# Gated linear attention on one core: the gate's split parts stacked as rows of one product, values and output gates as 512-column products, and the mixer's steps in another order

## The chip, the cores and the metric
The kernel runs on one core of a Trainium2 chip. The metric is device time in microseconds (us), the median of three runs; lower is better.

## The reference
A bidirectional encoder of four layers over 256 tokens of width 1024. Each layer is a half-step SwiGLU feed-forward network (FFN, inner width 2816), one mixer, and a second FFN, each with RMSNorm ahead and a residual add behind. The fourth layer's mixer is the one that the change touches, a gated linear attention (GLA) with 4 heads (keys 128 wide, values 256 wide) in both directions:

```python
def _gla_mixer(u, w_in, w_a1, w_a2, b_a, norm_g, w_o):
    proj = u @ w_in
    q, k, v, r = jnp.split(proj, [GLA_DK, 2 * GLA_DK, 2 * GLA_DK + GLA_DV], axis=-1)
    ...
    def log_decay(d):
        z = ((u @ w_a1[d]) @ w_a2[d] + b_a[d]).astype(F32)
        return (jax.nn.log_sigmoid(z) / GLA_TAU).reshape(b, s, GLA_HEADS, GLA_HEAD_K)
    ...
    o = o_fwd + o_bwd
    o = o * lax.rsqrt(jnp.mean(o * o, axis=-1, keepdims=True) + EPS)
    o = o.reshape(b, s, GLA_DV) * norm_g.astype(F32) * jax.nn.silu(r.astype(F32))
    return o.astype(u.dtype) @ w_o
```

`w_a1` is 1024 x 16 and `w_a2` 16 x 512 for each direction; each direction is a scan over chunks of 64 tokens with a masked product inside a chunk.

## The kernel before
**Products.** Every large product is made of float32r parts: an operand is split into a rounded part (ACT, Copy, `split` L634 and `split_block` L167) and the rest (DVE, subtract, L636 and L170), and a product is three matmuls (`mm3`), or in the FFN a 256-column and a 512-column one (`wide`). TensorE (PE) holds 128 x 128 weights and streams 256 or 512 columns.

**Weights.** SP loads blocks of 128 x 2048 numbers (1 MB) into a ring of 4 (`raw`), ACT and DVE split each into a ring of 4 (`w`), the stage's code takes a block with `take`, gives it back with `done`, and `pump` issues the splits that are owed. A new block is loaded when one has been split, so splits, loads and PE's demand move together.

**Order.** There is no planner: each engine works through its instructions in the order in which the code issues them, and a wait stands where the code put it. A tile with a tag has `bufs` buffers; the next tile with the tag waits until the readers of the one that it replaces are done. The eight PSUM banks form two halves of four, here called A0 to A3 and B0 to B3. `ab()` goes round one half and leaves out the banks in `held`; `dbank(j)` names a bank of the other half. The mixer's `bank()` alternates between the two until the output product has begun (`D4`, made by the first `dmm`), which keeps the four `dbank` banks; from there on only the four of `ab()` are left.

**What lies ahead of the mixer.** The FFN before it runs eleven column steps: `take_up("w1", i)` into the banks PA, `take_up("w3", i)` into the banks PB, each evacuated by two ACT copies (`parts`, L466) and two DVE adds (`add`, L471); then DVE multiplies (L474, L480), ACT takes the silu, and the gate's result `g` is split. At i = 4 the code calls `pre3` (L1150), which loads and prepares the mixer's small operands: the gate's first weights `was`, the triangles `tri` and `lst`, `mask`, and the gate's second weights `wa2`. They come through tiles with the tag `craw` (2 buffers), which POOL (GpSimd) clears and fills by DMA and ACT and DVE convert; `wa2` is loaded as it is.

**The mixer** (`mix3`, L1180): `qkproj` 0 to 3 make queries and keys, evacuated by DVE (`qkevac`, L1222 and L1225); the gate's first product with `was` stands between 1 and 2; the four gate products (`gate_a`, L1252, fp32, 17 rows with the bias as a row of ones) stand among the steps of `qkproj(2)`; ACT and DVE turn them into log decays (`gate_b`, `gate_c`). Then each head has `vproj` and `rproj` (8 steps each, one block of weights, one bank; evacuated by ACT, L1289 and L1309) and `decays`, `states`, `scores`, `out`, `trans`, which are spread among these steps by `fill` so that PE has work while ACT and DVE prepare what it needs next. `dmm` is a step of the output product.

## Time and profile before
| | before |
|---|---|
| runs (us) | 1937.98, 1934.15, 1933.92 |
| median (us) | 1934.15 |
| profiled execution (us) | 1937.17 |
| its span (us) | 1935.0 |
| mean granted clock of TensorE, share of full | 0.994 |
| PE busy | 1906.1 us, 99% |
| DVE busy | 1397.5 us, 72% |
| ACT busy | 995.4 us, 51% |
| POOL busy | 35.0 us, 2% |

The page gives for each engine the time in which it executed something, for each group of instructions the mean duration and the idle time of the engine just before them with what ended it, and the chain of work that ended last. The timeline gives single instructions with their start and duration (a run of equal ones is one row with its count; a row's duration runs to the end of its last one). The profiled execution is one run, 3.0 us over the median.

### The profile page before, as it was taken

How to read it: one execution, taken by the hardware profiler on the slowest of the kernel's cores; microseconds unless marked ns; L12 is line 12 of the kernel's file. 1: busy time of each engine (PE TensorE's matmuls, PEld its weight loads, DVE VectorE, ACT ScalarE, POOL GpSimd, SP SyncE). 2: the span in 40 equal slices, each digit the busy share in tenths (PEclk: the TensorE clock that was granted, in tenths of full speed). 3: DMA queues.
4: the chain of work that ended last, by engine and by line, in shares of the span. 5: the costliest groups of instructions: out<-in, count | busy, mean ns of one | idle time of the engine just before them, and what ended most of it. 6: DMA issues, size and time to landing. Idle time of an engine off the chain costs nothing.

```text
span 1935.0 us, 29203 instructions
## 1 busy us (share of the span) xinstructions
PE 1906.1 (99%) x12272; PEld 1683.3 (87%) x12272; DVE 1397.5 (72%) x1850; ACT 995.4 (51%) x1273; POOL 35.0 (2%) x55
## 2 busy tenths in 40 slices
PE   7999999999999999899999999999999999999998
PEld 6888999888888898788888889988888888998886
DVE  7776567876687767787668776687777766768774
ACT  6554444655455544555545544555445455756452
POOL 0000000000040000000000000000000000000000
PEclk9999999999999999899999999999999999999999
DMA  7655533465445543245545544365546553335550
GB/s 264 219 194 193 188 131 131 153 217 196 174 164 212 194 162 144 79 163 216 196 174 196 195 176 164 133 226 183 183 168 220 201 196 111 131 130 193 199 196 22
DMA packets 48644, 338.10 MB, mean 175 GB/s; under 512 B 5568, under 2 KB 5744, under 8 KB 8192
## 3 DMA queue, kind: packets, MB, share of 16 engines
q1 hardware_dynamic: 47952, 335.11, 48.3%
q8 instruction: 96, 1.57, 0.3%
q0 software_dynamic: 560, 1.12, 0.2%
q14 instruction: 36, 0.29, 0.0%
HBM read 335.16 MB, written 1.05 MB: 174 GB/s over the span
## 4 chain that ended last, share of the span: by engine, by line
PE 92%; DVE 5%; ACT 2%; DMA 1%; issue 1%; SPq 0%; DVEq 0%; ACTq 0%
PE B L81 50%; PE A L81 41%; DVE w L170 1%; ACT w L167 1%; DVE zc L765 1%; DMA raw<-in_ffn_w_dram 0%; PE A L84 0%; DMA h<-in_x_dram 0%; ACT zc L880 0%; PE B L84 0%; DVE h L279 0%; DVE acc L355 0%; DVE x L304 0%; DVE sl L474 0%; ACT x L302 0%
## 5 line engine op out<-in xcount | busy, mean ns | idle before, releaser
L170 DVE TENSOR_TENSOR w<-raw,w 128x2048 fp32r<-128x2048 f32 x315 | 720.4, 2293 | 289.7 <-ACT w L167 289.4
L167 ACT ACTIVATE w<-raw 128x2048 fp32r<-128x2048 f32 x315 | 598.8, 1909 | 109.0 <-PE A L81 47.4
L81 PE MATMUL B<-x,w 128*128 128x256 f32 (+1 forms) x3968 | 643.5, 322 | 1.4 <-DVE sl L471 1.2
L81 PEld LDWEIGHTS B<-x,w 128*128 128x128 f32 x3968 | 571.5, 190 | 71.1 <-issue 5.5
L81 PE MATMUL A<-x,w 128*128 128x256 f32 x3008 | 522.4, 335 | 10.9 <-DVE w L636 7.3
L81 PEld LDWEIGHTS A<-x,w 128*128 128x128 f32 x3008 | 455.5, 189 | 74.9 <-DVE w L636 7.3
L81 PE MATMUL B<-g,w 128*128 128x256 f32 (+1 forms) x1408 | 251.1, 336 | 0.3 <-DVE w L170 0.2
L81 PE MATMUL A<-g,w 128*128 128x256 f32 (+1 forms) x1408 | 250.3, 336 | 0.0
L81 PEld LDWEIGHTS B<-g,w 128*128 128x128 f32 x1408 | 216.5, 187 | 32.2 <-DVE g L636 0.5
L81 PEld LDWEIGHTS A<-g,w 128*128 128x128 f32 x1408 | 216.6, 187 | 31.4
L635 ACT ACTIVATE g<-br 128x512 fp32r<-128x512 f32 x88 | 55.6, 632 | 252.9 <-DVE br L480 252.9
L474 DVE TENSOR_TENSOR sl<-sl,R 128x512 f32<-128x512 f32 x176 | 121.9, 696 | 2.5
L636 DVE TENSOR_TENSOR g<-br,g 128x512 fp32r<-128x512 f32 x88 | 61.1, 695 | 61.4 <-ACT g L635 61.4
L302 ACT ACTIVATE x<-h,cols 128x256 fp32r<-128x256 f32 x88 | 39.9, 501 | 68.3 <-DVE h L279 49.0
L466 ACT ACTIVATE br<-B 128x256 f32<-128x256 f32 x88 | 30.3, 385 | 76.3 <-PE B L81 76.3
L477 ACT ACTIVATE sl<-sl 128x512 f32<-128x512 f32 x88 | 55.0, 627 | 24.5 <-DVE sl L474 24.4
L466 ACT ACTIVATE br<-A 128x256 f32<-128x256 f32 x88 | 30.2, 384 | 71.5 <-PE A L81 71.4
L81 PE MATMUL B<-w,x 128*128 128x256 f32 (+1 forms) x504 | 62.6, 284 | 0.0
L81 PEld LDWEIGHTS B<-w,x 128*128 128x128 f32 x504 | 61.3, 191 | 0.4 <-issue 0.3
L480 DVE TENSOR_TENSOR br<-sl,br 128x512 f32<-128x512 f32 x88 | 60.7, 690 | 0.5
L466 ACT ACTIVATE sl<-A 128x256 f32<-128x256 f32 x88 | 29.8, 377 | 53.1 <-PE A L81 53.1
L466 ACT ACTIVATE sl<-B 128x256 f32<-128x256 f32 x88 | 29.9, 378 | 51.5 <-PE B L81 51.1
(293 smaller groups left out, 1088.9 us busy)
## 6 DMA issues: line engine op xcount, KB each, us to landing
raw<-in_ffn_w_dram SPq DMA_DIRECT2D x262, 1024.0 KB, 4.8
raw<-in_attn_w_qk_dram SPq DMA_DIRECT2D x12, 1024.0 KB, 4.8
raw<-in_conv_w_pw_dram SPq DMA_DIRECT2D x12, 1024.0 KB, 4.8
raw<-in_gla_w_in_dram SPq DMA_DIRECT2D x12, 1024.0 KB, 4.8
raw<-in_attn_w_v_dram SPq DMA_DIRECT2D x6, 1024.0 KB, 4.8
raw<-in_fnet_w_dram SPq DMA_DIRECT2D x4, 1024.0 KB, 4.8
raw<-in_gla_w_o_dram SPq DMA_DIRECT2D x4, 1024.0 KB, 4.7
raw<-in_ffn_w_dram SPq DMA_DIRECT2D x8, 256.0 KB, 6.1
```

The source lines that it names most:

```text
L81: return self.nc.tensor.matmul(out, lhsT, rhs, start=start, stop=stop, skip_group_check=True)
L167: self.nc.scalar.activation(w[:, 0], raw, AF.Copy)
L170: (eng or self.nc.vector).tensor_tensor(w[:, 1], raw, f32(w[:, 0]), ALU.subtract)
L302: nc.scalar.activation(xh[:, c], h[:, c], AF.Copy, scale=g[c])
L466: nc.scalar.activation(t[:, c], P[c][:, 1], AF.Copy)
L474: nc.vector.tensor_tensor(t, t, self.Rb(), ALU.mult)
L477: nc.scalar.activation(t, t, AF.Silu)
L480: nc.vector.tensor_tensor(br, sl, br, ALU.mult)
L635: self.nc.scalar.activation(p[:, 0], src, AF.Copy)
L636: self.nc.vector.tensor_tensor(p[:, 1], src, f32(p[:, 0]), ALU.subtract)
L765: nc.vector.scalar_tensor_tensor(o, x, w, o, ALU.mult, ALU.add)
```

## The change
In `pre3` the tag `craw` has one buffer in place of two. `was` has 128 columns in place of 64 (four groups of 32: for each direction the weights twice) and is loaded and split in two halves, each a clearing and four DMAs; `wa2` becomes a pair of float32r parts, 128 x 512, made from a cleared tile with eight small DMAs; it now stands ahead of the triangles and the mask. The gate's input `t1` has 128 rows; its rounded part and rest become the rows of one operand `t2`, so that a gate is two float32r products of 64 and 32 rows in place of one fp32 product of 17 rows. `vproj` and `rproj` become `vrproj`: blocks of 4 x 512 columns (`gla_w_vr`, laid out by the host), two banks per head, 512-column matmuls, 48 per head in place of 96 of 256 columns; values and output gates of a head are evacuated together at its end (L1310, L1313), and the values lie in the space of `was`. The steps are spread by counts (6; then 4, 2, 2; for the last head 12, 4, 6 steps of the output product), and the output product begins right behind the decays of head 3.

```diff
     def pre3(self):
 
         nc, P = self.nc, self.prepool
-        raw = lambda shape: self.sb(self.ev, shape, F32, "craw", 2)
-
-        wa = raw([128, 8, 64])
-        nc.gpsimd.memset(wa, 0.0)
-        for d in range(2):
-            nc.gpsimd.dma_start(wa[:, :, 32 * d:32 * d + 16],
-                                self.a["gla_w_a1"][0, d].rearrange("(k p) n -> p k n", p=128))
+        raw = lambda shape: self.sb(self.ev, shape, F32, "craw", 1)
+
+        was = self.pair(P, [128, 8, 128], "was")
+        cut = [slice(32 * n + 1, 32 * n + 17) for n in range(4)]
+        for ks in (slice(0, 4), slice(4, 8)):
+            wa = raw([128, 4, 128])
+            nc.gpsimd.memset(wa, 0.0)
+            for n, c in enumerate(cut):
+                nc.gpsimd.dma_start(wa[:, :, c],
+                                    self.a["gla_w_a1"][0, n // 2].rearrange("(k p) n -> p k n", p=128)[:, ks])
+            self.split(wa, was[:, :, ks])
+
+        wb = raw([128, 512])
+        nc.gpsimd.memset(wb, 0.0)
+        for n, c in enumerate(cut):
+            nc.gpsimd.dma_start(wb[c, :], self.a["gla_w_a2"][0, n // 2])
+            nc.gpsimd.dma_start(wb[32 * n:32 * n + 1, :], self.a["gla_b_a"][0, n // 2:n // 2 + 1, :])
+        wa2 = self.pair(P, [128, 512], "wa2")
+        self.split(wb, wa2)
         traw = raw([128, 2, 256])
         nc.gpsimd.dma_start(traw, self.a["c_tri"])
-        was = self.pair(P, [128, 8, 64], "was")
-        self.split(wa, was)
         tri = self.sb(P, [128, 2, 256], F32R, "tri")
         nc.scalar.activation(tri, traw, AF.Copy)
         lraw = raw([128, 2, 128])
@@ -1171,10 +1181,6 @@
         nc.scalar.activation(lst, lraw, AF.Copy)
         mask = self.sb(P, [128, 2, 256], mybir.dt.uint8, "mask")
         nc.vector.tensor_copy(mask, mraw)
-        wa2 = self.sb(P, [64, 512], F32, "wa2")
-        for d in range(2):
-            nc.gpsimd.dma_start(wa2[32 * d:32 * d + 16, :], self.a["gla_w_a2"][0, d])
-            nc.gpsimd.dma_start(wa2[32 * d + 16:32 * d + 17, :], self.a["gla_b_a"][0, d:d + 1, :])
         return was, wa2, tri, lst, mask
...
-                self.held = [self.nab]
+                self.held = self.held + [self.nab]
...
         for k in range(8):
-            self.mm3(pa[0:64, 0:256], was[:, :, k], self.xk(k), start=k == 0, stop=k == 7)
+            self.mm3(pa[:, 0:256], was[:, :, k], self.xk(k), start=k == 0, stop=k == 7)
         self.bcast()
-        t1 = T([64, 256])
-        nc.gpsimd.memset(t1, 1.0)
+
+        t1 = T([128, 256])
+        t2 = T([128, 256], F32R, "t2", 1)
+        nc.vector.tensor_tensor(t1, pa[:, 0:256], self.R, ALU.mult)
         for d in range(2):
-            pr = slice(32 * d, 32 * d + 16)
-            nc.vector.tensor_tensor(t1[pr], pa[pr, 0:256], self.R[pr], ALU.mult)
+            nc.gpsimd.memset(t1[64 * d:64 * d + 1], 1.0)
+        nc.scalar.activation(t2, t1, AF.Copy)
+        for d in range(2):
+            pr = slice(64 * d + 32, 64 * d + 64)
+            nc.vector.tensor_tensor(t2[pr], t1[pr], f32(t2[pr]), ALU.subtract)
         qkevac(0, p0)
         qkevac(1, p1)
 
+        v = f32(self.pair(self.prepool, [128, 8, 128], "was")).rearrange("p t a b -> p t (a b)")
+        vt = [v[:, t] for t in range(2)]
+
 
...
         def gate_a(d, t):
-            pr = slice(32 * d, 32 * d + 17)
             p = bank()
-            self.mm(p, t1[pr, 128 * t:128 * t + 128], wa2[pr, :], start=True, stop=True)
+            for n in range(2):
+                pr = slice(64 * d, 64 * d + (64, 32)[n])
+                self.mm(p, t2[pr, 128 * t:128 * t + 128], wa2[pr, n], start=n == 0, stop=n == 1)
             az = self.sb(ev, [128, 512], F32, f"ks{d}{t}")
...
 
-        def vproj(i):
+        rg = {}
+
+        def vrproj(i):
 
             def step(k, s):
+                if k % 4 == 0:
+                    s["w"] = self.take(("gvr", i, k // 4))
                 if k == 0:
-                    s["w"], s["p"] = self.take(("gv", i)), bank(True)
+                    s["p"] = [bank(True) for _ in range(2)]
                 w, p = s["w"], s["p"]
                 for t in range(2):
-                    self.mm3(p[:, 256 * t:256 * t + 256], self.xk(k, t), w[:, :, k],
-                             start=k == 0 and t == 0, stop=k == 7)
+                    x = self.xk(k, t)
+                    for n, (a, b) in enumerate(((0, 0), (0, 1), (1, 0))):
+                        self.mm(p[t], x[:, a], w[:, b, k % 4], start=k == 0 and n == 0, stop=k == 7 and n == 2)
+                if k % 4 == 3:
+                    self.done()
                 if k == 7:
                     self.held = []
-                    self.done()
-                    for t in range(2):
-                        nc.scalar.activation(vt[t][:, 256 * i:256 * i + 256], p[:, 256 * t:256 * t + 256], AF.Copy,
-                                             scale=self.rc[:, t:t + 1])
-            s = {}
-            return [lambda k=k: step(k, s) for k in range(8)]
-
-        rg = {}
-
-        def rproj(i):
-            def step(k, s):
-                if k == 0:
-                    s["w"], s["p"] = self.take(("gr", i)), bank(True)
-                w, p = s["w"], s["p"]
-                for t in range(2):
-                    self.mm3(p[:, 256 * t:256 * t + 256], self.xk(k, t), w[:, :, k],
-                             start=k == 0 and t == 0, stop=k == 7)
-                if k == 7:
-                    self.held = []
-                    self.done()
                     g = self.sb(ev, [128, 2, 256], F32, "rg", 2)
                     for t in range(2):
-                        nc.scalar.activation(g[:, t], p[:, 256 * t:256 * t + 256], AF.Silu, scale=self.rc[:, t:t + 1])
+                        nc.scalar.activation(vt[t][:, 256 * i:256 * i + 256], p[t][:, 0:256], AF.Copy,
+                                             scale=self.rc[:, t:t + 1])
+                    for t in range(2):
+                        nc.scalar.activation(g[:, t], p[t][:, 256:512], AF.Silu, scale=self.rc[:, t:t + 1])
                     rg[i] = g
             s = {}
             return [lambda k=k: step(k, s) for k in range(8)]
@@ -1433,44 +1437,31 @@
             for _ in range(len(steps) if n is None else n):
                 steps.pop(0)()
 
-        fill(vproj(0))
         H = [head(hd) for hd in range(4)]
-        f = rproj(0)
-        fill(f, 4)
+        f = vrproj(0)
+        fill(f, 6)
         kstate()
-        H[0][0]()
         fill(f)
-        H[0][1]()
-        self.pump(1)
-        f = vproj(1)
-        fill(f, 4)
-        H[0][2]()
-        self.pump()
-        fill(f)
-        H[0][3]()
-        for hd in range(1, 4):
+        for hd in range(4):
             decays, states, scores, out, trans = H[hd]
             decays()
             self.pump()
-            f = rproj(hd)
             if hd < 3:
-                fill(f)
-                states()
-                H[hd - 1][4]()
-                f = vproj(hd + 1)
-                fill(f, 4)
-                scores()
+                f = vrproj(hd + 1)
+                n = (4, 2, 2)
             else:
-                fill(f, 4)
-                states()
-                fill(f)
-                scores()
-                H[2][4]()
                 wo = [self.take(("go", j)) for j in range(2)]
                 f = [lambda j=j, k=k, d=d: self.dmm(wo[j], og[j], d, k)
                      for j in range(2) for k in range(2) for d in (4, 5, 6, 7, 0, 1, 2, 3)]
+                n = (12, 4, 6)
+            fill(f, n[0])
+            states()
+            if hd:
+                H[hd - 1][4]()
+            fill(f, n[1])
+            scores()
             self.pump()
-            fill(f, 4)
+            fill(f, n[2])
             out()
         fill(f)
...
+
+    w = a["gla_w_in"][0]
+    o["gla_w_in"] = cols(w[:, :1024], 4)[0]
+    o["gla_w_vr"] = w[:, 1024:].reshape(2, 4, 128, 2, 4, 256).transpose(4, 0, 2, 1, 3, 5).reshape(4, 2, 128, 2048)
```

Three places in the engines' queues. The first is ACT's queue at `pre3`, ahead of the mixer, between the FFN's silu of step 4 (`sl`) and the evacuation of the step's `w3` product (`br`); `DMASW` is a wait for a DMA that POOL issued. Before:

```order
L477 ACTIVATE sl_1008_12792<-sl_1008_12792 128x512 [waits DVE_49]
L635 ACTIVATE was_1013_12810<-craw_1011_12804 128x512 [waits DMASW5_49,DMASW4_49,Pool_49]
L1165 ACTIVATE tri_1014_12813<-craw_1012_12808 128x512 [waits DMASW6_49]
L1171 ACTIVATE lst_1017_12819<-craw_1015_12815 128x256 [waits DMASW7_49]
L466 ACTIVATE br_1020_12860<-A2_71 128x256 [waits PE_49]
L466 ACTIVATE br_1020_12860<-A3_72 128x256 [waits PE_49]
L167 ACTIVATE w_1021_12863<-raw_1000_12667 128x2048 [waits DMAHW5_49,Activation_49]
```

With the change:

```order
L477 ACTIVATE sl_1008_12792<-sl_1008_12792 128x512 [waits DVE_49]
L635 ACTIVATE was_1011_12804<-craw_1012_12805 128x512 [waits DMASW6_49,DMASW5_49,DMASW7_49,DMASW4_49,Pool_49]
L635 ACTIVATE was_1011_12804<-craw_1013_12813 128x512 [waits DMASW2_49,DMASW1_49,DMASW3_49,DMASW0_49,Pool_49]
L635 ACTIVATE wa2_1015_12831<-craw_1014_12821 128x512 [waits DMASW4_49,DMASW3_49,DMASW5_49,DMASW2_49,DMASW6_49,DMASW1_49,DMASW7_49,DMASW0_49,Pool_49]
L1175 ACTIVATE tri_1017_12836<-craw_1016_12834 128x512 [waits DMASW4_49]
L1181 ACTIVATE lst_1020_12842<-craw_1018_12838 128x256 [waits DMASW5_49]
L466 ACTIVATE br_1022_12878<-A2_71 128x256 [waits PE_49]
L466 ACTIVATE br_1022_12878<-A3_72 128x256 [waits PE_49]
L167 ACTIVATE w_1023_12881<-raw_1000_12667 128x2048 [waits DMAHW5_49,Activation_49]
```

Three conversions stood ahead of the evacuation `br`; now five do, each with its own buffer generation of `craw` and its own landing.

The second is PE's queue at head 0, around the decays (`tri` with the log decays `la`); `w` with `x` are the steps of the projections, `lst` and `kT` belong to `kstate`. Before:

```order
L81 MATMUL B0_73<-w_1107_14001,x1_1075_13599 128x256 x12
L84 MATMUL A3_72<-ident_105,kT_1096_13844 128x128 x2
...
L81 MATMUL B3_76<-la11_1116_14088,lst_1017_12819 128x512
L81 MATMUL A2_71<-tri_1014_12813,la00_1113_14079 128x256 [waits Activation_49]
L81 MATMUL A2_71<-tri_1014_12813,la00_1113_14079 128x256
L81 MATMUL A2_71<-tri_1014_12813,la01_1114_14082 128x256 x2
L81 MATMUL B1_74<-tri_1014_12813,la10_1115_14085 128x256 [waits Activation_49]
L81 MATMUL B1_74<-tri_1014_12813,la10_1115_14085 128x256
L81 MATMUL B1_74<-tri_1014_12813,la11_1116_14088 128x256 x2
L81 MATMUL B0_73<-w_1107_14001,x2_1087_13796 128x256 x12
L81 MATMUL B0_73<-w_1107_14001,x3_1089_13824 128x256 x12
L81 MATMUL A3_72<-gv0_1097_13845,ks00_1123_14235 128x256 [waits DVE_49]
```

With the change:

```order
L80 MATMUL A2_71<-w_1106_14016,x0_1076_13599 128x512 [waits Activation_49]
L80 MATMUL A2_71<-w_1106_14016,x0_1076_13599 128x512 x2
L80 MATMUL B0_73<-w_1106_14016,x0_1076_13599 128x512 [waits DVE_49]
L80 MATMUL B0_73<-w_1106_14016,x0_1076_13599 128x512 x2
...
L80 MATMUL B3_76<-la11_1118_14113,lst_1020_12842 128x512
L80 MATMUL A2_71<-w_1108_14021,x3_1091_13842 128x512 x3
L80 MATMUL B0_73<-w_1108_14021,x3_1091_13842 128x512 x3
L80 MATMUL A2_71<-w_1108_14021,x3_1091_13842 128x512 x3
L80 MATMUL B0_73<-w_1108_14021,x3_1091_13842 128x512 x3
L80 MATMUL A2_71<-tri_1017_12836,la00_1115_14104 128x256 [waits Activation_49]
L80 MATMUL A2_71<-tri_1017_12836,la00_1115_14104 128x256
L80 MATMUL A2_71<-tri_1017_12836,la01_1116_14107 128x256 x2
L80 MATMUL B0_73<-tri_1017_12836,la10_1117_14110 128x256 [waits Activation_49]
```

The decays stood in the middle of head 0's output-gate steps (bank B0) and wrote A2 and B1, from which the values had gone long before; now they stand right behind the last step of head 0 and write A2 and B0, the two banks that this step has just filled. The second bank, B0, is also the one of `qkproj(2)`, with a wait for DVE at its first matmul.

The third is PE's queue from the output of head 2 (`P` and `S`) over the decays of head 3 to what follows. Before:

```order
L81 MATMUL A1_70<-S12_1193_14721,E1_1182_14641 64x256
L81 MATMUL B0_73<-tri_1014_12813,la00_1113_14079 128x256 x2
L81 MATMUL B0_73<-tri_1014_12813,la01_1114_14082 128x256 x2
L81 MATMUL A2_71<-tri_1014_12813,la10_1115_14085 128x256 x2
L81 MATMUL A2_71<-tri_1014_12813,la11_1116_14088 128x256 x2
L81 MATMUL B1_74<-w_1170_14563,x0_1074_13581 128x256 x12
L81 MATMUL B1_74<-w_1170_14563,x1_1075_13599 128x256 x12
L81 MATMUL A3_72<-gv0_1097_13845,ks00_1123_14235 128x256 [waits Activation_49]
L81 MATMUL B2_75<-gv0_1097_13845,ks00_1123_14235 128x256
```

With the change:

```order
L80 MATMUL B3_76<-S12_1197_14631,E1_1187_14578 64x256
L80 MATMUL A2_71<-tri_1017_12836,la00_1115_14104 128x256 [waits Activation_49]
L80 MATMUL A2_71<-tri_1017_12836,la00_1115_14104 128x256
L80 MATMUL A2_71<-tri_1017_12836,la01_1116_14107 128x256 x2
L80 MATMUL B0_73<-tri_1017_12836,la10_1117_14110 128x256 x2
L80 MATMUL B0_73<-tri_1017_12836,la11_1118_14113 128x256 x2
L80 MATMUL A2_71<-og0_1159_14411,w_1174_14509 128x256 [waits Activation_49]
L80 MATMUL A2_71<-og0_1159_14411,w_1174_14509 128x256 x5
L80 MATMUL A3_72<-og0_1159_14411,w_1174_14509 128x256 x6
...
L80 MATMUL A3_72<-og0_1159_14411,w_1174_14509 128x256 x6
L80 MATMUL B1_74<-was_1110_14027,ks00_1125_14222 128x256
```

Behind the decays stood four steps of a projection into the free bank B1; now the output product (`og`) starts there, in A2, which the decays have just filled.

## Rows read from the trace of the kernel before

**Rows 1.** The page, part 1: busy time of each engine

```profile
PE 1906.1 (99%) x12272; PEld 1683.3 (87%) x12272; DVE 1397.5 (72%) x1850; ACT 995.4 (51%) x1273; POOL 35.0 (2%) x55
```

**Rows 2.** The page, part 4: the chain that ended last

```profile
PE 92%; DVE 5%; ACT 2%; DMA 1%; issue 1%; SPq 0%; DVEq 0%; ACTq 0%
```

**Rows 3.** Timeline, FFN ahead of the mixer: start, duration, engine, line, out<-in [idle before <-releaser]

```profile
1479.01 0.63 ACT L635 ACTIVATE was<-craw 128x512 fp32r<-128x512 f32 x1
...
1480.85 0.68 DVE L636 TENSOR_TENSOR was<-craw,was 128x512 fp32r<-128x512 f32 x1
...
1481.83 0.54 POOL L1169 DMA_DIRECT2D craw<-in_c_mask_dram  x1 [0.82 <-DVE was L636]
...
1483.35 0.48 POOL L1176 DMA_DIRECT2D wa<-in_gla_w_a_dram  x1
...
1486.76 0.43 DVE L1173 CAST mask<-craw 128x512 uint8<-128x512 f32 x1 [5.22 <-DMA craw<-in_c_mask_dram]
...
1486.98 18.19 PE L81 MATMUL A<-x,w 128*128 128x256 f32 x104
...
1487.70 0.74 DVE L471 TENSOR_TENSOR br<-br,A 128x256 f32<-128x256 f32 x2
...
1495.96 0.74 DVE L471 TENSOR_TENSOR sl<-sl,A 128x256 f32<-128x256 f32 x2
```

**Rows 4.** Timeline, POOL at its first loads for the mixer

```profile
1423.79 0.53 POOL L1156 MEMSET craw<- 128x512 f32 x1 [706.90 <-DVE acc L355]
...
1424.61 1.83 POOL L1158 DMA_DIRECT2D craw<-in_gla_w_a_dram  x2 [0.29 <-POOL craw L1156]
```

**Rows 5.** Windows: length, clock, share of the DMA engines, GB/s

```profile
1484.00:1485.00 1.00, 1.00 1.05 434
```

**Rows 6.** DMA issues, 1400 to 1800 us: KB each, us to landing

```profile
craw<-in_c_mask_dram POOLq DMA_DIRECT2D x1, 256.0 KB, 4.9
craw<-in_gla_w_a_dram POOLq DMA_DIRECT2D x2, 64.0 KB, 3.8
craw<-in_c_tril_dram POOLq DMA_DIRECT2D x1, 128.0 KB, 2.3
```

**Rows 7.** Timeline, a head's 48 matmuls of 256 columns, then `states` and its evacuation

```profile
1684.09 5.91 PE L81 MATMUL A<-w,x 128*128 128x256 f32 x48
...
1689.93 0.48 PE L81 MATMUL B<-gv,ks 64*128 64x256 f32 x1
...
1692.18 0.86 DVE L1376 SCALAR_TENSOR_TENSOR S<-S,dc,B 128x256 f32<-128x256 f32 x2
```

**Rows 8.** Timeline, a gate's product, DVE's evacuations of queries and keys

```profile
1623.26 1.12 PE L81 MATMUL A<-wa,t 17*128 17x512 f32 x2
...
1626.40 0.68 DVE L1222 SCALAR_TENSOR_TENSOR qT<-B,R 128x512 f32<-128x512 f32 x1
...
1639.99 1.28 DVE L1225 TENSOR_TENSOR kT<-B,R 128x512 f32<-128x512 f32 x2
```

**Rows 9.** Windows: length, PE busy, granted clock, share of the DMA engines, GB/s

```profile
1628.40:1632.00 3.60, 3.60 (x9) 0.50 0.71 287
1632.00:1635.20 3.20, 3.20 (x16) 0.50 0.00 0
...
812.60:816.00 3.40, 3.33 (x16) 0.50 0.58 246
```

**Rows 10.** Timeline, PE in the conv mixer, ahead of the last of these windows

```profile
812.29 12.11 PE L81 MATMUL A<-zs,w 128*128 128x256 f32 x84 [2.35 <-ACT zs L635]
```

**Rows 11.** Timeline, heads 0 and 1: output gates, decays behind an output, their evacuation

```profile
1654.93 1.28 ACT L1309 ACT_TABLE_LOAD   x1
...
1656.22 0.84 ACT L1309 ACTIVATE rg<-B,rc 128x256 f32<-128x256 f32 x2
...
1665.15 0.74 PE L81 MATMUL B<-tri,la 128*128 128x256 f32 x4
...
1667.91 0.38 ACT L1351 ACTIVATE Em<-B 128x256 f32<-128x256 f32 x1
```

More of the change, by code (lines that the diff above doesn't have):

```diff
@@ L23 @@
 NW = 4
-GLA_ORDER = [("gv", 0), ("gr", 0), ("gv", 1), ("gr", 1), ("gv", 2), ("gr", 2), ("gv", 3), ("gr", 3)]
 ALL_STAGES = [s for i in range(4) for s in (("ffn", i, 0), ("mix", i), ("ffn", i, 1))]
@@ L141, in plan @@
                     add(("gqk", i), a["gla_w_in"][i], 8)
-                for n, i in GLA_ORDER:
-                    add((n, i), a["gla_w_in"][{"gv": 4, "gr": 8}[n] + i], 8)
+                for i in range(4):
+                    for hf in range(2):
+                        add(("gvr", i, hf), a["gla_w_vr"][i, hf], 4)
                 for j in range(4):
@@ L1204, in mix3 @@
         kT = self.sb(ev, [128, 4, 256], F32, "kT")
-        vt = [self.sb(ev, [128, 1024], F32, f"gv{t}") for t in range(2)]
         def qkproj(i, hook=None):
@@ L1603, in lay @@
     o["conv_w_pw1"] = cols(a["conv_w_pw1"], 8)[0]
-    o["gla_w_in"] = cols(a["gla_w_in"], 12)[0]
+    w = a["gla_w_in"][0]
+    o["gla_w_in"] = cols(w[:, :1024], 4)[0]
+    o["gla_w_vr"] = w[:, 1024:].reshape(2, 4, 128, 2, 4, 256).transpose(4, 0, 2, 1, 3, 5).reshape(4, 2, 128, 2048)
     for n in ("attn_w_o", "conv_w_pw2", "gla_w_o"):
```

## The prediction
> **What bounds the kernel now.** I read the page first: PE is busy for 1906.1 of 1935.0 us [rows 1], and the chain that ended last lies on PE for 92% [rows 2]. So PE's time is the kernel's time: work taken from PE is a gain if PE does not then wait, and every new wait of PE is a loss, whatever DVE (72%) and ACT (51%) have to spare over the whole. The timeline then shows two stretches that the change touches, the FFN step in which `pre3` stands and the mixer. In both I looked for the next event that PE needs and the queue behind which it stands. Two things are to be seen there. ACT and DVE work strictly in their order: DVE stood still for 5.22 us until the mask had landed, although the evacuation of a finished bank (`br`, L471) was behind it [rows 3]. That idle time cost PE nothing: the add began at 1487.70, and PE came to that bank only after 32 more matmuls. And a buffer with the tag `craw` is filled again only when its last reader is done: the mask's DMA waited for DVE's read of `was` [rows 3].
>
> **1. `pre3`, the largest term.** One buffer for six loads makes one chain: clear, load, convert, and only then the next load. The first load has been there for long, as now. From the end of DVE's part of it the chain is, by rows: DVE done 1480.85 + 0.68 = 1481.53 [rows 3]; 0.3 to POOL, a clearing 0.53, 0.29 to the DMA [rows 4]; four DMAs. An issue takes 0.92 for two halves of 64 KB [rows 4] and 0.48 for a small one [rows 3]; for 32 KB I take 0.7, so that the last begins at 1484.75.
>
> The landing is the unknown. Three rows bound it: 2.3 for 128 KB, 3.8 for 64 KB, 4.9 for 256 KB [rows 6]. The size does not order them. The 4.9 fell together with a weight block, while the DMA engines moved 434 GB/s [rows 5]. In the chain no new block is loaded, since blocks are loaded when one has been split and ACT and DVE split nothing while they stand there; only the block on its way until some 1486 is in the way. So I take 2.9 for the second half of `was`, 2.3 for the small ones, 2.65 for the two of 256 KB (2.3 and 128 KB more at that rate), 2.3 for `tril`; together 12.8. If all took 2.3 it would be 11.5, if all took 4.9, 24.5.
>
> The clock goes on: landed 1487.65; ACT 0.63 and DVE 0.68 [rows 3], 1489.0; clearing and hops as above 1490.1; eight DMAs of 0.48, the last begins at 1493.5, landed 1495.8; converted 1497.15; `tri` 0.3 later, landed 1500.1, converted 1500.75; `tril` landed 1503.35, converted (0.4) 1503.8; the mask landed 1506.75, converted by DVE. In the trace `br`'s add began 0.94 after the mask's conversion [rows 3], so now at 1507.7, and its first half is done at 1508.1.
>
> PE's cover: the row of 104 matmuls has 174.9 ns each [rows 3]; the 32 of `w1` end at 1486.98 + 5.6 = 1492.6, and the next one writes the bank that `br` holds. **PE stands for 15.5 us.** Behind it DVE is late: it took 8.26 us from `br`'s add to the next `sl` add [rows 3], PE has only the 5.6 us of `w3` until it needs that bank: 8.26 + 0.37 - 0.4 - 5.6 = 2.6. **Together 18.1** (16.8 to 29.8 by the landings).
>
> **2. The gate.** Four gates lay on PE with 1.12 us each [rows 8]; now each is two 512-column matmuls. The pair of 256 and 512 columns takes 349.8 ns (twice 174.9), the 256-column one 5.84 / 48 = 121.7, from the start of a head's 48 to the start of the next work [rows 7], so a 512-column one 228 and a gate, with the same tail of 0.07, 0.54: -2.3. Besides, PE ran at half clock in both windows from 1628.4 to 1635.2 [rows 9], behind gates that use 17 rows: 6.8 us, 3.4 lost. With 64 and 32 rows in half the time I take this stretch as gone (0 if it comes again): -3.4.
>
> What is late next: the fourth gate writes the bank of `qkproj(1)`, whose evacuation (`qT`, 1626.40, [rows 8]) stands behind two splits of weights on DVE. These now stand behind a longer preparation: one product, a clearing of two rows by POOL, an ACT copy, two DVE subtractions, some 2.1 us more. So the bank is free at about 1629.2, and PE, some 3 us earlier, comes at 1626.9: +2.4. Then the first product of `vrproj(0)` takes B0, the bank of `qkproj(2)`, which DVE frees with `kT` behind all log decays: 1639.99 + 0.64 [rows 8], by my count of ACT's chain 1 us earlier now. Before, the first product went to another bank. PE comes at 1636.3: +3.3. So the gate's gain on PE is given back at once: ACT and DVE set the pace between gate and `kT`.
>
> **3. 512 columns.** Each of eight products of 48 x 256 columns becomes 24 x 512: 5.84 - 24 x 0.228 = 0.37, together -2.9 (0 if a 512-column matmul costs twice a 256-column one). The Trainium skill ("TensorE: Matmul & The Clock Gate", on back-to-back issue at full clock) gives N/2.4 GHz and 2.5 ns; by an estimate from this the two are 109.2 and 215.7 ns, the gain would be 0.5 and my sum 2.4 higher. The trace's 121.7 ns for 256 columns does not agree, and I go by it.
>
> **4. The banks of the new order.** `vrproj` fills two banks, and ACT empties them after the last step in this order: two copies, a table load of 1.28, two silus of 0.42 each [rows 11]. A bank is free with its silu: 0.2 + 0.84 + 1.28 + 0.44 = 2.75 after PE's last matmul, less a little that PE has left: 2.6 for `decays(0)`, which follow directly in A2, and 2.5 each for `out(1)` and `out(2)`, which follow directly in the first bank of the next head's pair; 0.1 for `decays(1)`, which have an output ahead. Before, rg's bank was never the next one wanted. The Trainium skill ("ScalarE: Activation LUTs", what a table load costs) counts 1380 ns of draining besides 1283 for the load; by it each of the three waits would be 1.4 longer. Here the silu begins 1.29 after the load's start, so no row shows it.
>
> Head 3: the first `dmm` writes A2, which the decays have just filled; Em is read 1667.91 + 0.38 - 1665.15 = 3.1 after the decays began [rows 11], PE is there after 1.0: +2.1. `states` now fill all four banks left, and `trans(2)` follows at once: S is done 1692.18 + 0.86 - 1689.93 = 3.1 after the states began [rows 7], which take 1.5: +1.6. `trans(3)` has less output work ahead: +0.7, an estimate. Sum: 2.4 + 3.3 + 2.6 + 0.1 + 2.5 + 2.5 + 2.1 + 1.6 + 0.7 = **17.8**.
>
> **5. The clock.** Behind a wait of 2.35 us [rows 10] PE ran at half clock (1.2 GHz) for 3.4 us [rows 9], 1.7 lost. Part 2 and part 4 bring six waits of that size; I count two such stretches, +3.4 (0 to +10.2). Behind the long wait in the FFN it costs nothing more, since PE waits for DVE there again.
>
> `was` has 128 columns as weights in place of 64 and streams the same 256; the moved `wa2` and POOL's clearing of `t1` are in the chains above. Edits in the host's layout cost nothing: the blocks are of 1 MB and as many as before, behind the same ring.
>
> **The sum.** 18.1 + 17.8 - 2.3 - 3.4 - 2.9 + 3.4 = +30.7. The profiled execution took 1937.17, 3.0 over the median of 1934.15; against its own time this is 1967.9, against the median 1964.9. I predict **1965**; its own range is 1957 to 1975.
>
> **Rivals.**
> - *The loads are as slow as the slowest row.* 4.9 each, 11.7 more: 1977. For it: two of the three landings in the rows are 3.8 and over. Against: a weight block lay beside them. Some of it is likelier than all.
> - *All six waits bring half clock.* 6.8 more: 1972.
> - *`pre3` stays hidden* (the chain runs earlier than I think, or PE has more to do than `w1`): without 18.1, 1947. It decides if `br`'s add ends before 1492.6. Against: ACT's queue holds all five conversions ahead of `br`.
> - *A table load holds ACT 1.4 us longer* in part 4, by its price for draining: three times, 1969. The row above speaks against it.
> - *ACT and DVE keep ahead of PE: faster.* The place is the queues behind each new wait; the price is that of the waits. If every landing and every evacuation were over when PE comes, only the gains were left, 2.3 + 3.4 + 2.9 = 8.6: 1925.5. It decides as soon as the new waits together are under 8.6 us. For it: ACT is busy for half the span only. Against: the silus come behind PE's last matmul into the very bank that PE wants next, whatever ACT did before.
> - *512 columns bring nothing*: 2.9 more, 1968.
>
> **How the numbers follow.** My forecast 0.62; slow landings in full or in part 0.13; half clock everywhere 0.1; hidden `pre3` 0.06; the table load 0.02; no gain from 512 columns 0.04; faster 0.03. The range takes the forecast's own and the cases above it and leaves out the hidden `pre3` and the faster case: 1952 to 1979. A measurement of this kernel tells some 0.2%, 3.9 us, from no change; the forecast lies eight times that away, and only the last big rival lies below. Faster 0.03, same 0.01, slower 0.96.
>
> **What would show it.** Right: ACT and DVE idle for most of 1481 to 1508 with releasers DMA `craw`, POOL with a row of `craw` every few us, PE idle for some 15 us ahead of an A bank in `w3`, released by DVE L471; in the mixer PE idle behind ACT `rg` three times, DVE `qT`, DVE `kT`, ACT `Em`, DVE `S`; no half clock around the gates. Wrong: PE's wait in the FFN under 8 or over 25 us; silu waits under 1 us; a half clock behind every wait.

## The result and the profile after

The changed kernel takes 1966.42 us in the median (1964.64 to 1967.42) against 1934.68 before: a ratio of 1.0159, with a 95% interval of 1.0147 to 1.0172, 31.7 us slower. The forecast was 1965 with a range of 1952 to 1979.

The page of the changed kernel, part 1, shows that PE did as much as before [rows 1] and that only the span grew:

```profile
PE 1906.3 (97%) x12080; PEld 1674.2 (85%) x12080; DVE 1398.7 (71%) x1853; ACT 999.7 (51%) x1278; POOL 42.5 (2%) x68
```

The view of PE's waits, 1400 to 1800 us of the changed kernel, by what ended them (total in us, times, longest), names the waits that the change brought:

```profile
PE A L80 <- DVE br L471: 15.1, 1, 15.1
PE A L80 <- ACT rg L1313: 4.9, 2, 2.6
PE B L80 <- DVE kT L1230: 2.6, 1, 2.6
PE B L80 <- ACT rg L1313: 2.3, 1, 2.3
PE A L80 <- ACT Em L1355: 2.0, 1, 2.0
PE B L83 <- DVE S L1380: 1.8, 1, 1.8
...
PE B L80 <- DVE qT L1227: 0.2, 1, 0.2
```

The same view of the kernel before has one line:

```profile
PE B L81 <- DVE sl L471: 0.2, 1, 0.2
```

The largest stands in the FFN ahead of the mixer. The timeline of the changed kernel there (start, duration, engine, line, out<-in, idle before and its releaser) is the chain that answers to [rows 3]:

```profile
1478.64 0.53 POOL L1159 MEMSET craw<- 128x512 f32 x1 [53.53 <-DVE was L636]
1479.46 2.96 POOL L1161 DMA_DIRECT2D craw<-in_gla_w_a_dram  x4 [0.29 <-POOL craw L1159]
...
1484.34 0.63 ACT L635 ACTIVATE was<-craw 128x512 fp32r<-128x512 f32 x1 [7.65 <-DMA craw<-in_gla_w_a_dram]
1485.01 0.69 DVE L636 TENSOR_TENSOR was<-craw,was 128x512 fp32r<-128x512 f32 x1 [6.43 <-ACT was L635]
...
1491.94 0.63 ACT L635 ACTIVATE wa<-craw 128x512 fp32r<-128x512 f32 x1 [6.96 <-DMA craw<-in_gla_b_a_dram]
...
1496.51 0.63 ACT L1175 ACTIVATE tri<-craw 128x512 fp32r<-128x512 f32 x1 [3.94 <-DMA craw<-in_c_tri_dram]
...
1499.82 0.42 ACT L1181 ACTIVATE lst<-craw 128x256 fp32r<-128x256 f32 x1 [2.68 <-DMA craw<-in_c_tril_dram]
...
1503.45 0.43 DVE L1183 CAST mask<-craw 128x512 uint8<-128x512 f32 x1 [10.16 <-DMA craw<-in_c_mask_dram]
...
1504.40 0.74 DVE L471 TENSOR_TENSOR br<-br,A 128x256 f32<-128x256 f32 x2
1504.87 8.09 PE L80 MATMUL A<-x,w 128*128 128x256 f32 x32 [15.14 <-DVE br L471]
```

Read it from top to bottom: each conversion on ACT or DVE waited for a landing (the idle times 7.65, 6.96, 3.94, 2.68, 10.16), each load for the conversion above it, and PE stood for 15.14 us until DVE, done with the mask, came to the add of `br`. The landings in the view of the DMA issues (KB each, median us) answer to [rows 6]:

```profile
craw<-in_gla_w_a_dram POOLq DMA_DIRECT2D x12, 32.0 KB, 2.5
craw<-in_c_tri_dram POOLq DMA_DIRECT2D x1, 256.0 KB, 2.9
craw<-in_c_mask_dram POOLq DMA_DIRECT2D x1, 256.0 KB, 2.9
craw<-in_c_tril_dram POOLq DMA_DIRECT2D x1, 128.0 KB, 2.4
craw<-in_gla_b_a_dram POOLq DMA_DIRECT2D x4, 2.0 KB, 1.8
```

### The profile page after: what moved, and what is told of

Its sections match the earlier page's. It is cut to its first block, busy times and chain, and to the rows that moved or that the text cites. A ratio compares the mean times of both kernels' runs of the same rounds, so it can differ in the third digit from the quotient of the medians.

```text
span 1962.7 us, 28853 instructions
## 1 busy us (share of the span) xinstructions
PE 1906.3 (97%) x12080; PEld 1674.2 (85%) x12080; DVE 1398.7 (71%) x1853; ACT 999.7 (51%) x1278; POOL 42.5 (2%) x68
## 5 line engine op out<-in xcount | busy, mean ns | idle before, releaser
L80 PE MATMUL A<-x,w 128*128 128x256 f32 x3008 | 525.0, 336 | 26.8 <-DVE br L471 15.1
L80 PEld LDWEIGHTS A<-x,w 128*128 128x128 f32 x3008 | 458.0, 190 | 90.8 <-DVE br L471 15.5
L80 PE MATMUL B<-w,x 128*128 128x256 f32 (+2 forms) x408 | 66.0, 310 | 2.6 <-DVE kT L1230 2.6
L80 PEld LDWEIGHTS B<-w,x 128*128 128x128 f32 x408 | 56.0, 192 | 6.8 <-DVE kT L1230 3.0
```

What stands on the lines that cost most here:

```text
L80: return self.nc.tensor.matmul(out, lhsT, rhs, start=start, stop=stop, skip_group_check=True)
```

## The experiments

Each is timed beside the kernel before on the same chip; medians of that one were 1934.98 to 1935.30. Waits and half clock are read from one profiled execution of each.

**Six buffers for the loads (e1).** In the changed kernel's `pre3`:

```diff
-        raw = lambda shape: self.sb(self.ev, shape, F32, "craw", 1)
+        raw = lambda shape: self.sb(self.ev, shape, F32, "craw", 6)
```

> The changed kernel, with six buffers for the tag craw in place of one, so that the six loads of pre3 need not wait for each other; nothing else is different. Chain theory (the changed kernel loses its time ahead of the mixer to loads that follow each other through one buffer): PE's wait of 15.14 us ahead of the w3 product of step 5 is gone, and with it the half clock behind it (17.07 us at half in the changed kernel, of which some 2.4 us fall on work); the time falls by about 17.5 us, from 1966.4 to 1949. Rival (the conversions themselves hold ACT and DVE: five on ACT with 0.63 us each and four on DVE with 0.69 instead of three and two): they stay behind each other and PE still waits some us; 1953 or more. Second rival (the loads only trade places with the weight blocks, whose splits are then late): PE waits for w instead, 1955 or more.

Measured: 1951.9 us. The timeline shows all loads issued by 1436, the five conversions on ACT and four on DVE back to back, and the add of `br` in time:

```profile
1477.27 1.15 ACT L635 ACTIVATE was<-craw 128x512 fp32r<-128x512 f32 x2
...
1480.91 0.42 DVE L1183 CAST mask<-craw 128x512 uint8<-128x512 f32 x1
...
1481.85 0.74 DVE L471 TENSOR_TENSOR br<-br,A 128x256 f32<-128x256 f32 x2
...
1485.23 15.07 PE L80 MATMUL A<-x,w 128*128 128x256 f32 x86
```

The wait of 15.14 is gone, and hardly anything comes in its place (PE waits 0.8 us for adds of `sl`, in place of 0.4); 14.5 of the 17.5 us are won. The missing 3 are, by the profile, the clock's: behind the mixer's waits PE now ran at half clock four times, in the changed kernel twice (below).

**Two buffers (e11).** The same line with 2.

> The changed kernel with two buffers for the tag craw, as the kernel before had; nothing else is different. Chain theory: both halves of was are there early, as now only the first; wa2 is filled while ACT and DVE convert, tri follows behind its eight DMAs on POOL, tril behind wa2's conversion, mask behind tri's. By the changed kernel's own rows (DMAs 0.48 and 0.57, landings 1.8 to 2.9, conversions 0.4 to 0.7) the mask is converted some 10 to 12 us earlier than there; PE's wait of 15.14 us falls to 3 to 5, and the next add is still late by some 1 to 2: 1966.4 - 11 = 1955, between e1 (1951.9) and the changed kernel. Rival (the number of loads and conversions counts, not the buffers): 1964 or more. Rival (two buffers hide the chain in full): 1952.

Measured: 1954.63. PE waits 2.3 us for `br`, less than the 3 to 5 expected, and 0.87 for the next add. With 1, 2 and 6 buffers PE's wait for `br` is 15.1, 2.3 and 0: the buffers make the time, the number of loads does not.

**The kernel before with one buffer (e2).**

```diff
-        raw = lambda shape: self.sb(self.ev, shape, F32, "craw", 2)
+        raw = lambda shape: self.sb(self.ev, shape, F32, "craw", 1)
```

> The kernel before, with one buffer for the tag craw in place of two; nothing else is different. Chain theory: the loads of tri, tril and mask follow each other. From DVE's end with was at 1481.5 on: tri lands after 2.9 to 4.9 us, converted 0.63, tril 2.4, converted 0.42, mask 2.9, converted, the add of br 0.94 later, with 0.3 between each: its first half ends at 1493.0 to 1495.0, where PE wants the bank at 1492.6. So PE waits 0.4 to 2.4 us, and up to 2.6 us behind it for the next add: 1935 to 1940, 1938 likeliest. Rival (one buffer is dear in itself, however few the loads): 1945 or more. Rival (short chains are hidden altogether): 1934.7.

Measured: 1943.02 (single runs 1937.34 to 1944.27; ratio 1.0032, 1.0019 to 1.0044), above the 1935 to 1940 that were expected and below the rival's 1945. The timeline of this kernel:

```profile
1482.01 0.56 POOL L1161 DMA_DIRECT2D craw<-in_c_tri_dram  x1 [55.39 <-DVE was L636]
...
1486.56 0.64 ACT L1165 ACTIVATE tri<-craw 128x512 fp32r<-128x512 f32 x1 [6.74 <-DMA craw<-in_c_tri_dram]
...
1493.69 0.43 DVE L1173 CAST mask<-craw 128x512 uint8<-128x512 f32 x1 [11.98 <-DMA craw<-in_c_mask_dram]
...
1495.10 7.44 PE L81 MATMUL A<-x,w 128*128 128x256 f32 x32 [2.24 <-DVE br L471]
```

The mechanism is there, with a wait at the upper end of what was expected (2.24, and 0.83 behind it), since `tri`, started beside a weight block, took 4.5 us to land, where it takes 2.9 without one. That makes 3.1 of the 7.0 that lie between the two profiled executions (1944.18 and 1937.17); half clock behind the wait (32 matmuls at 1495.10 in 7.44 us in place of 5.7) and a longer stretch of it at the gates (10.2 us in place of 6.8) make 3.4 more, and 0.5 is open. The prediction of this run had left the clock out.

**Copies ahead of the silu (e3).**

```diff
                     for t in range(2):
                         nc.scalar.activation(vt[t][:, 256 * i:256 * i + 256], p[t][:, 0:256], AF.Copy,
                                              scale=self.rc[:, t:t + 1])
-                    for t in range(2):
-                        nc.scalar.activation(g[:, t], p[t][:, 256:512], AF.Silu, scale=self.rc[:, t:t + 1])
+                        nc.scalar.activation(g[:, t], p[t][:, 256:512], AF.Copy, scale=self.rc[:, t:t + 1])
+                    nc.scalar.activation(g, g, AF.Silu)
```

> The changed kernel, with another evacuation of vrproj: ACT copies values and raw output gate of the first bank, then of the second, and applies the silu afterwards in the buffer, so that a bank is free before the table load (one ACT instruction more per head). Theory of the banks (PE waits for the first bank's silu, that is for a table load in front of it): the three waits behind ACT rg, 2.56, 2.34 and 2.34 us, fall to 0.4 to 0.7 each; the half clock behind the first of them (1670.3 to 1673.7) goes too; together 5.5 to 7 us, less some 0.4 by the later table load ahead of the decays' exponentials, which Em of head 3 must wait for: 1960 to 1961.5. Rival (ACT as a whole is late there, and PE would only wait elsewhere, for E, S or the weights): at most 2 us gained, 1964.4 or more.

Measured: 1959.43, 7.0 us less. The three waits behind `rg` are 0.78, 0.25 and 0.25 in place of 2.56, 2.34 and 2.34, and in the profiled execution PE was at half clock nowhere in the mixer. That execution was the fastest of the four (1955.9; mean granted clock 0.992, the others 0.989 to 0.992). The view of PE's waits in this kernel has

```profile
PE A L80 <- ACT rg L1312: 1.0, 2, 0.8
...
PE B L80 <- ACT rg L1312: 0.3, 1, 0.3
```

**Another bank at the start of `vrproj(0)` (e5).**

```diff
                 if k == 0:
+                    if i == 0:
+                        self.ab()
                     s["p"] = [bank(True) for _ in range(2)]
```

> The changed kernel, with the second bank of vrproj(0) one further in the ring: B1, which the gates leave, in place of B0, which qkproj(2) holds until kT is evacuated; the later banks of this half move by one. Theory of the banks: PE's wait of 2.60 us for DVE kT at the start of vrproj(0) is gone and nothing takes its place, since kT is next wanted six steps later; 1966.4 - 2.7 = 1963.7. Rival (PE only comes earlier to log decays that ACT and DVE have not finished, or to weight blocks not split): the wait appears ahead of the products of la with lst or of the second block, and the time stays at 1966.

Measured: 1963.88. The wait for `kT` is gone and no other has come in the mixer, 2.5 us less than the changed kernel.

**The output product's first bank last (e4).**

```diff
-                     for j in range(2) for k in range(2) for d in (4, 5, 6, 7, 0, 1, 2, 3)]
+                     for j in range(2) for k in range(2) for d in (6, 7, 0, 1, 2, 3, 4, 5)]
```

> The changed kernel, with the output product's columns taken in another order (6, 7, 0, 1, 2, 3, 4, 5 in place of 4 to 7 and 0 to 3), so that its first steps write the bank A3 and the bank of the decays of head 3, A2, comes last, some 2.2 us later, when Em has been read; nothing else is different. Theory of the banks (each wait stands for itself, as the prediction added them): PE's wait of 1.98 us for ACT Em is gone, 1966.4 - 2.0 = 1964.4. Rival (the end of the mixer hangs on one chain, from the decays of head 3 over Em, S and P to its output, and PE runs out of other work whatever it waits for): the wait for S grows by about 1.9, from 1.85 to 3.7, and the time stays at 1966.

Measured: 1969.68. The wait for Em is gone, the one for S has grown, as the rival had it:

```profile
PE B L83 <- DVE S L1380: 3.4, 1, 3.4
```

The two were 1.98 and 1.85 and are now 3.40 in one: at the end of the mixer PE waits for one chain through head 3, and which bank it asks for first only decides where. The time lies above both expectations, 3.3 over the changed kernel; in its profile PE ran at half clock in the mixer for five stretches' length in place of two.

**All of these together (e7).** e1, e3, e5 and e4, and besides, for head 3,

```diff
-            if hd:
+            if 0 < hd < 3:
                 H[hd - 1][4]()
             fill(f, n[1])
+            if hd == 3:
+                H[2][4]()
             scores()
```

with `n = (12, 6, 4)` there.

> The changed kernel with the edits of e1 (six buffers), e3 (copies first), e5 (other bank) and e4 (order of the output product) together, and the transposes of head 2 behind six steps of the output product in place of ahead of four. By e1, e3 and e5, each against 1966.4: -14.5, -7.0, -2.5; the last two edits 0 (if the end of the mixer is one chain) to -3.8 (if its waits stand alone): 1942.4 to 1938.6. Theory of the waits (what the change takes from PE is there, and only new waits hide it): with all waits gone it would reach 1934.7 less 7 us of gains, 1928. Rival (DVE and ACT are the bound of the mixer once PE's work is shorter, so that a wait taken away comes again elsewhere): above 1940, with other waits for DVE.

Measured: 1935.15, ratio to the kernel before 0.9998 (0.9989 to 1.0007). The gains of e1, e3 and e5 alone, 14.5, 7.0 and 2.5, would make 1942.4; the 7 more come with the order around head 3 (Em and S waited for 3.83, S and `P` now for 1.7) and with the clock, as this mixer has no half clock, where e5 still had two stretches and e1 four. How the rest of the 7 divides I did not separate. It is not the 1928 of the first theory. The view of PE's waits in this kernel, in the mixer:

```profile
PE B L83 <- DVE S L1382: 1.1, 1, 1.1
PE A L80 <- ACT rg L1314: 1.0, 2, 0.8
PE B L80 <- DVE P L1393: 0.6, 1, 0.6
...
PE B L80 <- ACT rg L1314: 0.2, 1, 0.2
```

What that costs is read beside e9 (next), which has the same gate and the order of before. From the product with `was` (1615.87 here, 1614.18 there) to the output product of head 3, PE takes 87.86 us here; there it takes 81.80 and has the last projection's 48 matmuls still to do, 2.96 and 2.98 in its two halves: 87.74, nearly the same. Behind it PE takes 20.18 here (1703.73 to 1723.91) and 23.12 - 5.94 = 17.18 there (1695.98 to 1719.10), 3.0 less. Two timelines of PE show why, e7 first:

```profile
1709.68 2.41 PE L80 MATMUL A<-og,w 128*128 128x256 f32 x18
1713.18 0.63 PE L83 MATMUL B<-ident,t 128*128 128x128 f32 x4 [1.08 <-DVE S L1382]
...
1714.45 1.67 PE L80 MATMUL A<-og,w 128*128 128x256 f32 x12
1716.73 1.13 PE L80 MATMUL B<-was,P 128*128 128x256 f32 x4 [0.61 <-DVE P L1393]
```

and e9 at the same work:

```profile
1700.43 3.14 PE L81 MATMUL B<-w,x 128*128 128x256 f32 x24
1703.41 1.05 PE L81 MATMUL A<-E,Em 128*128 128x128 f32 x8
...
1704.65 1.65 PE L81 MATMUL A<-og,w 128*128 128x256 f32 x12
1706.30 1.10 PE L81 MATMUL B<-was,P 128*128 128x256 f32 x4
```

The output product alone does not last through head 3's chain of S, Em and `P`; the order of before has a projection left there and waits for none of them. So the 3.2 that 512 columns gave are gone, up to there, into the waits for `rg` and `qT`, 1.4, and into smaller pieces that I have not split, and the order loses another 3 at its end. The 512-column products in the order of before were not tried.

**The gate alone, on the kernel before (e9).** The change's `pre3` with six buffers and its gate, with

```diff
             p = bank()
+            if d and t:
+                p = self.dbank(3)
             for n in range(2):
                 pr = slice(64 * d, 64 * d + (64, 32)[n])
```

> The kernel before with the change's gate alone: its pre3 (with six buffers for craw, so that no chain is there), its stacked operands and its two products of 64 and 32 rows per gate; the values lie in the space of was, as in the change; the fourth gate writes the bank A3, which nobody holds, in place of the one that waits for qT. Projections, order of the steps and all the rest as before. Theory (the gate's part is a gain where its waits are avoided): the gates take 0.86 in place of 1.05, -0.8; the half clock of 6.8 us around them goes, -3.4; some 1 us given back where kstate then waits for kT: 1934.7 - 3.2 = 1931.5. Rival (between gate and kT ACT and DVE set the pace, so PE only waits longer): 1934.7. Rival (the half clock comes somewhere else near): 1934.

Measured: 1932.08, ratio 0.9982 (0.9974 to 0.9991): 3.2 us faster than the kernel before, and so a version that beats both. From the first gate to `rproj(0)` PE takes 17.73 us (1621.12 to 1638.85), before it took 21.58 (1623.26 to 1644.84). Most of that gain is the clock: the runs of the kernel before had a mean granted clock of 0.992 to 0.996, those of e9 0.995 to 0.997, and where both had 0.996, they took 1933.1 and 1932.2 on average, which leaves 0.9, near the 0.8 of the four shorter gates. In the two profiled executions e9 lacks the half clock around the gates (6.8 us), but also a stretch of 3.4 in the conv mixer [rows 9], which the edit does not touch; so how much of the 3.2 is the gate's is open. The window of this kernel from 1600 to 1650 (length, PE busy, clock) has neither idle time nor half clock:

```profile
1600.00:1650.00 50.00, 50.00 (x380) 1.00 0.33 127
```

**The gate with 128 rows (e10).** As e9, with an operand of 128 rows for each direction, zero in the other one's rows:

```diff
-                pr = slice(64 * d, 64 * d + (64, 32)[n])
-                self.mm(p, t2[pr, 128 * t:128 * t + 128], wa2[pr, n], start=n == 0, stop=n == 1)
+                self.mm(p, t2[d][:, 128 * t:128 * t + 128], wa2[:, n], start=n == 0, stop=n == 1)
```

> As e9, but each gate's two products have 128 rows: the operand of a direction is a tile of its own, with zeros in the rows of the other direction and in the same places of wa2; the second product thereby takes the small parts of both operands too. Theory of the rows (a product with 64 or 32 rows moves its columns at half the pace, 0.43 us for 512 with the clock granted in full, against 0.23 with 128 rows): a gate falls from 0.86 to 0.47, 1.6 us on PE in all, of which the wait for kT takes a part: 1930 to 1931.5. Rival (the gates are slow for another reason, their weights or operands): 0.86 stays, and the time with it.

Measured: 1931.88. The timeline of PE at a gate's two 512-column matmuls and what follows, in the changed kernel:

```profile
1638.44 0.93 PE L80 MATMUL A<-wa,t 64*128 64x512 f32 x2
1639.30 0.97 PE L80 MATMUL B<-x,w 128*128 128x256 f32 x6
```

and in e10:

```profile
1621.08 0.63 PE L81 MATMUL A<-wa,t 128*128 128x512 f32 x2
1621.55 0.87 PE L81 MATMUL B<-x,w 128*128 128x256 f32 x6
```

0.86 us from start to start with 64 and 32 rows, 0.47 with 128: the time hangs on the rows. That the columns move at half the pace, as the theory had it, is not what the traces show. The view of the tile `wa` gives the first and the last start of the weight loads (PEld) and of the products (PE), in e9:

```profile
L81 PEld LDWEIGHTS A<-wa,t x6: 181/182/183, 1621.1 to 1626.8; 64*128 64x128 f32 x3, 32*128 32x128 f32 x3
L81 PE MATMUL A<-wa,t x6: 489/497/502, 1621.1 to 1626.8; 64*128 64x512 f32 x3, 32*128 32x512 f32 x3
```

and in e10:

```profile
L81 PEld LDWEIGHTS A<-wa,t x6: 187/188/192, 1621.0 to 1624.6; 128*128 128x128 f32 x6
L81 PE MATMUL A<-wa,t x6: 394/396/397, 1621.1 to 1624.9; 128*128 128x512 f32 x6
```

In e9 a load starts together with its product, in e10 0.1 to 0.2 us ahead of it, while PE is still at the product before. A load that is not hidden (0.18) is about the 0.20 by which a product of e9 is longer. In e9 the number of rows also changes from product to product (128, 64, 32, 128), so whether few rows or the change of rows keeps the load back was not separated. From one gate to the next it is 1.76 us in e9 (1621.12 to 1622.88) and 1.18 in e10 (1621.08 to 1622.26).

The time moved by 0.2 us only, which these runs can't tell from nothing. In the trace PE starts `rproj(0)` at 1637.16, 1.7 us ahead of e9 (1638.85), after one more wait of 0.40 for a split, and is still 1.9 ahead at 1888; there it has a stretch of half clock that e9's profile has not. Whether that is what eats the gain in the other runs was not tried.

## Why the prediction was right

**`pre3`.** The wait was put at 15.5, with 12.8 for the five landings. The trace has 15.14, and from the last issue to the conversion 2.63, 1.96, 2.92, 2.38 and 2.92, together 12.8; no landing was off by more than 0.34, and that the sums agree so closely is luck. The choice that decided it was to take a landing without a weight block beside it: 2.4 and 2.9 us here, against 4.9 in [rows 6] and 4.5 in e2 beside one. The Trainium skill ("DMA: Bandwidth & Descriptors", on the path from GpSimd) gives about 2.0 us and the bytes at 436 GB/s; by an estimate from this the two of 256 KB would take 2.6 and `tril` 2.3. The measured 2.9 and 2.4 are near, the 4.9 beside a block is not. The 2.6 of lateness behind the wait came in another form: PE ran at half clock through its next 32 matmuls (8.09 us in place of 5.70) and then waited only 0.16. "It costs nothing more" was right for that reason. From `pre3` to `qkproj(2)` the trace has +18.14 (15.18, and 2.96 by which this execution had come to `pre3` earlier; 2.3 of these it had by the end of the conv mixer, where the wait of [rows 10] was 1.55 this time with no half clock behind it); 18.1 had been forecast.

**The gate: the step that failed, though it cost the sum nothing.** "A 512-column one 228 and a gate 0.54" was taken from products of 128 rows. With 64 and 32 rows a gate took 0.86 from start to start, so the four gained 0.8 in place of 2.3. PE came to the fourth gate 1.7 us later than was put, 1.0 of it by three slower gates, and DVE had freed the bank 0.5 sooner; so the wait for `qT`, put at 2.4, was 0.16. That the two errors cancel is not all luck: ACT and DVE set the pace up to `kT`, as the text said, and PE took up the second bank of `vrproj(0)` 19.44 us after the start of `qkproj(2)`, before the first projection 19.59. The half clock around the gates did go.

**The banks.** Forecast and trace, in the order of the prediction: `kT` 3.3 and 2.60; `rg` 2.6, 2.5, 2.5 and 2.56, 2.34, 2.34; Em 2.1 and 1.98; S 1.6 and 1.85; `trans(3)` 0.7 and 0.16. e3 and e5 show that those for `rg` and `kT` are what they were taken for; e4 shows that Em and S were wrongly added as two, since they are one chain (their sum was right). The table load took 1.28 with the silu 1.29 behind its start, as before, so the rival with a draining time falls.

**512 columns.** Three matmuls take 0.68, 227 ns each: a head's 48 take 10.9 in place of 11.7, 0.8 less, 3.2 in all; 2.9 was forecast. By an estimate from the figures of the Trainium skill ("TensorE: Matmul & The Clock Gate", back-to-back issue) it would have been 0.5 in all; the trace does not agree.

**The clock.** Two stretches of 3.4 us were counted, and the profile has two, behind the waits for `rg` and Em. The view of windows of the changed kernel (length, PE busy, granted clock, share of the DMA engines, GB/s):

```profile
1654.00:1658.00 4.00, 3.90 (x17) 1.00 0.19 25
...
1670.30:1673.60 3.30, 3.30 (x13) 0.50 0.00 0
...
1731.80:1735.00 3.20, 3.20 (x15) 0.50 0.01 3
```

None followed the longest of the mixer's waits, 2.60 (first row), and in e1, where one followed that wait, there were four in all. So the number changes from kernel to kernel with the same waits in the mixer, two and four, 1.7 us each; that two were counted and two came is luck. The rival "all six waits" did not come true in this profile.

**The sum.** From `qkproj(2)` to the end the span grew by 328.03 - 315.53 = 12.5; forecast 12.6. The terms as measured make +14.0 (waits, one of 0.16 for `t` among them) - 0.8 - 3.4 - 3.2 + 3.4 = +10.0. Of the 2.5 that are missing, some 1.2 can be the part of each wait that the view doesn't count, as a matmul's duration runs 0.15 over the start of the next; the rest is not attributed. So the mixer's terms were right singly within 0.7, but for the gate and `qT`, and its sum is better than they are, which again is luck.

## What to carry to other kernels

Count the buffers of a staging tag against the loads that go through it: with one, each load pays its landing and both conversions in a row, and whatever stands behind the conversions on ACT and DVE pays with it. A longer product that fills two banks moves their evacuation into one burst; look at which bank PE asks for next, and put copies ahead of a function that needs a table load. And judge the parts singly: here a gate that with its clock was worth up to 3 us (e9) came together with a staging tag of one buffer that cost 14.5 (e1) and with banks and an order that cost the rest of the way to 32 us more.

## What the runs showed of the hardware

- Among products of 128 rows, a float32r product with 64 or 32 rows took 0.43 us for 512 columns with the clock granted in full (e9), one with 128 rows, zeros included, 0.23 (e10). With fewer rows the weight load began only with its own product.
- Waits of PE of 1.9 to 2.6 us were followed by half clock in some cases and not in others, with the same mixer and the same wait (2.6 for `kT`: half clock behind it in e1, none in the changed kernel; 1.9 at 1888 to 1890 us: half clock behind it in e10, none in e9). In e7 and e9, where the longest wait of PE from 1400 to 1800 us was 1.1 and 0.6, no half clock was left from 1400 to 1900 us.
- Half clock also came without a wait: in the kernel before around the fp32 gates of 17 rows ([rows 9], 6.8 us; in e2 10.2), where PE had waited for nothing. Around the float32r gates no profile shows it. Whether the rows or the type of the operands does it was not separated.
- A load of 256 KB by POOL landed in 2.9 us alone (the changed kernel) and in 4.5 to 4.9 beside one weight block of 1 MB (e2 and the kernel before).
